# The second product of a SwiGLU block: 8 of 22 inner blocks plainly, 14 by seven block products in one group

## The chip, the cores and the metric

One core of one Trainium2 chip runs the whole kernel. The metric is the device time of one execution in microseconds (us); less is better. Engines are named as in the profile: PE (matmuls), PEld (weight loads of PE), DVE (VectorE), ACT (ScalarE), POOL, and SP, whose queue issues the DMAs here.

## The reference

The kernel computes one decoder layer on 512 tokens of width 1024, in float32: a SwiGLU half-step, a mixing stage (retention and block-sparse attention, one input projection, one output projection), and a second SwiGLU half-step. The half-steps are what matters here:

```python
FFN_DIM = 2816
def _swiglu(h, w_gate, w_up, w_down):
    return (jax.nn.silu(h @ w_gate) * (h @ w_up)) @ w_down
x = x + 0.5 * _swiglu(_rms(x, ffn1_norm_w[l]), ffn1_w_gate[l], ffn1_w_up[l], ffn1_w_down[l])
...
x = x + 0.5 * _swiglu(_rms(x, ffn2_norm_w[l]), ffn2_w_gate[l], ffn2_w_up[l], ffn2_w_down[l])
```

In blocks of 128, the model width is 8 blocks and the inner width 22. The **gate and up products** make the 22 inner blocks `hs[0..21]` (each 128 by 512 tokens); the **down product** multiplies them with `w_down` to 8 output blocks.

## The kernel before

Each float32 operand is split in two float32r parts, a rounded `h` (an ACT copy) and a remainder `lo` (a DVE subtraction). A product then takes three matmuls: h·h, h·lo and lo·h (`mm3`, and the inner loop of `strassen`). Weights are loaded as 256 KB tiles `raw` (four 128x128 blocks), and split into `wh` and `wl`.

`ffn` runs once at the start (FFN1) and once at the end (FFN2). Its first 6 inner blocks (`EVEN`) are computed plainly, with moving tiles of 512 tokens. The other 16 go in 8 calls of `hidden`, each for two inner blocks, with the block method of seven products (Strassen's in Winograd's form): the matrix of weights is cut in 2 by 2, the tokens in two halves of 256, and seven products of 256 columns replace eight. A product of `hidden` has 24 matmuls (two weights matrices, four blocks deep, three parts), a call 168. `token_blocks` prepares the token side once (sums and differences of the normed input, and their splits), `strassen` the weight side in each call. `weave` interleaves two calls in time, so that products of one stand between products of the other. The results stay in PSUM banks: bank `a` takes P1 and then, added on top, U2, U3 and C21; bank `b` takes P5 and later B; bank `c` takes P2. What a bank holds after a product must be read before the next product adds to it: ACT copies it (`taken`, into `keep`).

The down product, which is the part in question, is plain in this version: for each of 8 output blocks `db`, 22 inner blocks by 3 matmuls of 512 columns, 66 in all, into one bank of `p` or `s` in turn; at its end one DVE instruction adds half of it to the residual `y`. In FFN2 the last output block is cut in two halves of 256 columns. All 22 inner blocks are split (`parts`). `nxt` then passes `y` on: in FFN1 to `Stream.add`, which makes the next norm's operands (on ACT a scaled copy and a square, on DVE a remainder and a sum), in FFN2 to a DMA to the output.

All operations are first recorded by `Plan` (line 71) and then ordered per engine by its list scheduler (`_order`), with assumed costs (`_cost`) and limits on live tiles (`SLOTS`, `BANKS`, 98 slots in all). Nearly every instruction therefore carries line 196 in the profile, where the recorded call is made. Engines work their queues strictly in that order.

Of the kernel before, what the change touches and what calls it, by code (L numbers as in the profile page):

```python
# [27 lines left out]
F32R = mybir.dt.float32r  # L28
# [6 lines left out]
KB = 8  # L35
# [282 lines left out]
def tile_layer(ctx: ExitStack, tc: tile.TileContext, x_t, cols_in, wg1, wu1, wd1, w_int, w_inn,  # L318
# [22 lines left out]
    def f32(ap):  # L341
        return ap.bitcast(F32)
# [87 lines left out]
    class Stream:  # L430


        def __init__(self, nw):
            self.nw, self.parts, self.ssq = nw, [], None

        def add(self, kb, x, delay=0):
            self.part(kb, x)
# [2 lines left out]
        def part(self, kb, x):  # L440
            w = self.nw[:, kb:kb + 1]
            h, lo = slot(F32R), slot(F32R)
            nc.scalar.activation(h, x, AF.Copy, scale=w)
            nc.vector.scalar_tensor_tensor(lo, x, w, f32(h), op0=OP.mult, op1=OP.subtract)
            self.parts.append((h, lo))

        def square(self, x, delay=0):
            nc.delay = delay
# [16 lines left out]
    def token_blocks(pairs, gates=None):  # L465


        res = [[] for _ in range(7)]
        gate = lambda q: setattr(nc, "after", gates and gates[min(q, len(gates) - 1)])
        for q, (one, two) in enumerate(pairs):  # L470
            gate(q)
            if q % 2 == 0:
                bh, bl = slot(F32R, use="block"), slot(F32R, use="block")
            o = slice(256 * (q % 2), 256 * (q % 2) + 256)
            nc.scalar.activation(bh[:, o], one[:, :256], AF.Copy)
            nc.vector.tensor_sub(bl[:, o], one[:, :256], f32(bh[:, o]))
            res[0].append((bh[:, o], bl[:, o]))
# [24 lines left out]
        return res  # L502

    def strassen(load, nk, moving, taken):

        n = nk * 128
        r = {}
        for i, j in ((1, 1), (1, 2), (2, 1), (2, 2)):  # L510
            r[i, j] = [slot(use="raw")[:, :n] for _ in range(2)]
            for m in range(2):
                load(r[i, j][m], m, i, j)

        s1 = [slot(use="sum")[:, :n] for _ in range(2)]
        s = [s1, s1, r[2, 1], r[1, 2]]
        for m in range(2):
            nc.vector.tensor_add(s1[m], r[2, 1][m], r[2, 2][m])
        for m in range(2):
            nc.vector.tensor_sub(s[2][m], r[1, 1][m], r[2, 1][m])  # L520
        banks, marks = {}, []

        def product(tag, w, block, said):
            start = tag not in banks
            if start:
                banks[tag] = bank(tag)
            p = banks[tag]
            marks.append(len(nc.ops) + 2)
            for m in range(2):
                h, lo = slot(F32R, use="wh")[:, :n], slot(F32R, use="wl")[:, :n]  # L530
                nc.scalar.activation(h, w[m], AF.Copy)
                nc.vector.tensor_sub(lo, w[m], f32(h))
                out = p[:, 256 * m:256 * m + 256]
                for k in range(nk):
                    o = slice(k * 128, k * 128 + 128)
                    xh, xl = moving[block][k]
                    for a, (ww, xx) in enumerate(((h, xh), (h, xl), (lo, xh))):
                        nc.tensor.matmul(out, ww[:, o], xx, start=start and m + k + a == 0,
                                         stop=k == nk - 1 and a == 2, skip_group_check=True)
# [8 lines left out]
        for m in range(2):  # L548
            nc.vector.tensor_sub(s1[m], s1[m], r[1, 1][m])
        product("a", s[1], 4, "U2")  # L550
        for m in range(2):
            nc.vector.tensor_sub(s[3][m], r[1, 2][m], s1[m])
# [27 lines left out]
    def ffn(st, x, wg, wu, wd, nxt, was, first=None, last=False):  # L580
# [40 lines left out]
        def hidden(one, two):  # L621
            def load(t, m, i, j):
                nc.sync.dma_start(t.rearrange("p (a b) -> p a b", a=4),
                                  (wg, wu)[m][(one, two)[i - 1]][:, 4 * j - 4:4 * j])

            rows = [[slot(use="row") for _ in range(2)] for _ in range(2)]
            keep = {}

            def add(i, j, p, old):

                for m in range(2):
                    o = slice(256 * m, 256 * m + 256)
                    nc.vector.tensor_add(rows[i][m][:, 256 * j:256 * j + 256], p[:, o], old[:, o])

            def taken(what, p):
                if what in ("P1", "U2", "U3"):
                    keep[what] = slot(use="keep")
                    nc.scalar.activation(keep[what], p, AF.Copy)
                elif what == "P5":
                    keep[what] = p  # L640
                if what == "P2":
                    add(0, 0, p, keep["P1"])
                elif what == "U3":
                    add(1, 1, keep["P5"], keep["U3"])
                    g, u = (t[:, 256:] for t in rows[1])
                    nc.scalar.activation(g, g, AF.Silu)
                    hs[two] = slot()
                    nc.vector.tensor_mul(hs[two][:, 256:], g, u)
                elif what == "C21":
                    g = rows[1][0][:, :256]  # L650
                    nc.scalar.activation(g, p[:, :256], AF.Silu)
                    nc.vector.tensor_mul(hs[two][:, :256], p[:, 256:], g)
                elif what == "B":
                    add(0, 1, p, keep["U2"])
# [5 lines left out]
            return strassen(load, 4, blocks, taken)  # L660

        marks = weave([lambda _, q=q: hidden(q, q + HALF) for q in range(EVEN, EVEN + HALF)])

# [3 lines left out]
            x[db] = slot()  # L667
            nc.sync.dma_start(x[db], was[db])
        nc.after = None
        order = [*range(FB - 1 - HALF), *range(FB - HALF, FB - 1), FB - 1 - HALF, FB - 1]  # L670
        parts = {}
        for fb in order:
            parts[fb] = split(hs[fb])
        for db in range(KB):

            cuts = [(0, 256), (256, 512)] if last and db == KB - 1 else [(0, 512)]
            ps = [bank("ps"[(db + i) % 2]) for i in range(len(cuts))]
            wh, wl = split_w(wd[db], (128, FB, 128))
            y = x[db]
            for p, (a, b) in zip(ps, cuts):  # L680
                for n, fb in enumerate(order):
                    hh, hl = parts[fb]
                    mm3(p[:, a:b], wh[:, fb], wl[:, fb], hh[:, a:b], hl[:, a:b], n == 0, n == FB - 1)
                nc.vector.scalar_tensor_tensor(y[:, a:b], p[:, a:b], 0.5, y[:, a:b],
                                               op0=OP.mult, op1=OP.add)
                nxt(db, y, a, b)

# [413 lines left out]
```

## Time and profile before

| | us |
|---|---|
| median of 3 runs (970.16 to 970.73) | 970.26 |
| profiled execution, whole | 970.63 |
| its span | 968.8 |
| PE busy (99% of the span, 5676 matmuls) | 960.1 |
| PEld busy (88%) | 848.3 |
| DVE busy (71%) | 687.1 |
| ACT busy (53%) | 510.1 |

The share of a span is a mean over stages. A row of a view by time gives the start, the duration, the engine, what it did, and in brackets the idle time before it with what ended that. A group of like instructions that follow each other without a gap stands as one row with a count, under the shape of the first; the last of them ends at start plus duration. The granted clock of PE stands in the views by window as PEclk, in parts of full speed. About 2 us of the whole lie outside the span.

### The profile page before, as it was taken

The numbers are of one execution on the slowest core, as the hardware profiler recorded it, in microseconds if no ns is written. First come the engines' busy times: TensorE is split into PE (matmuls) and PEld (weight loads), VectorE is DVE, ScalarE is ACT, GpSimd is POOL, SyncE is SP. The second block draws the span as 40 slices with busy tenths as digits, with TensorE's granted clock in tenths as the row PEclk, the third lists the DMA queues.
The fourth block names the chain that finished last, engine by engine and source line by source line (L and its number), as shares of the span: only waits on it lengthen the run. The fifth ranks groups of instructions, "written<-read, shape, count | busy, mean of one in ns | idle before, by whom it ended". The sixth has DMA issues, their size and how long they took to land.

```text
span 968.8 us, 15318 instructions
## 1 busy us (share of the span) xinstructions
PE 960.1 (99%) x5676; PEld 848.3 (88%) x5676; DVE 687.1 (71%) x1333; ACT 510.1 (53%) x999; POOL 0.2 (0%) x4
## 2 busy tenths in 40 slices
PE   9999999999999999999999999999999999999998
PEld 6889999999888888888788878888999999988888
DVE  7997888997343344379989988798788899733130
ACT  7544558556232235369987975554445765542200
POOL 0000000000000000000000000000000000000000
PEclk9999999999999999999999999999999999999999
DMA  9413332337425641114405432811333133643200
GB/s 307 174 55 103 107 97 77 97 106 226 134 83 184 184 150 36 58 66 117 159 27 164 158 103 70 273 60 54 110 101 111 54 109 108 199 149 125 87 28 22
DMA packets 65099, 112.24 MB, mean 116 GB/s; under 512 B 8064, under 2 KB 13184, under 8 KB 65024
## 3 DMA queue, kind: packets, MB, share of 16 engines
q1 hardware_dynamic: 65024, 111.26, 36.3%
q8 instruction: 44, 0.72, 0.3%
q14 instruction: 31, 0.25, 0.1%
HBM read 101.79 MB, written 6.29 MB: 112 GB/s over the span
## 4 chain that ended last, share of the span: by engine, by line
PE 87%; ACT 6%; DVE 4%; DMA 1%; issue 1%; SPq 1%; DVEq 0%; ACTq 0%
PE ps L196 87%; ACT s L196 6%; DVE s L196 4%; DMA s<-in_w_int_dram 1%; SPq L196 1%; DMA s<-in_x_t_dram 0%; DVE c L196 0%; DVE ad L196 0%; DVEq L196 0%; ACTq L196 0%
## 5 line engine op out<-in xcount | busy, mean ns | idle before, releaser
L196 PE MATMUL ps<-s 128*128 128x256 f32 (+1 forms) x5506 | 944.9, 332 | 3.1 <-ACT s L196 1.9
L196 PEld LDWEIGHTS ps<-s 128*128 128x128 f32 x5506 | 828.8, 190 | 105.5 <-ACT s L196 6.6
L196 DVE TENSOR_TENSOR s<-s 128x512 fp32r<-128x512 f32 (+5 forms) x834 | 498.3, 652 | 58.7 <-ACT s L196 50.2
L196 ACT ACTIVATE s<-s 128x512 fp32r<-128x512 f32 (+2 forms) x700 | 383.9, 603 | 222.6 <-DVE s L196 144.9
L196 DVE TENSOR_TENSOR s<-ps,s 128x256 f32<-128x256 f32 (+5 forms) x216 | 103.3, 501 | 44.8 <-PE ps L196 25.8
L196 ACT ACTIVATE s<-ps 128x512 f32<-128x512 f32 (+7 forms) x148 | 75.7, 519 | 84.5 <-PE ps L196 78.3
L196 DVE SCALAR_TENSOR_TENSOR s<-ps,s 128x512 f32<-128x512 f32 (+1 forms) x17 | 11.2, 660 | 144.0 <-PE ps L196 144.0
L196 ACT ACTIVATE s<-s,cols 128x512 fp32r<-128x512 f32 x24 | 17.2, 722 | 77.4 <-DVE s L196 75.9
L196 DVE SCALAR_TENSOR_TENSOR s<-s,cols 128x512 fp32r<-128x512 f32 (+1 forms) x44 | 32.1, 747 | 9.2 <-ACT s L196 8.9
L196 DVE SCALAR_TENSOR_TENSOR s<-s 128x512 f32<-128x512 f32 x30 | 20.6, 686 | 9.2 <-ACT s L196 8.9
L196 ACT ACTIVATE s<-s,c 128x384 f32<-128x384 f32 (+3 forms) x32 | 20.7, 649 | 1.7 <-DVE c L196 1.5
L196 PE MATMUL ps<-ct,s 128*128 128x128 f32 x100 | 17.3, 278 | 1.3 <-ACT s L196 1.3
L196 PEld LDWEIGHTS ps<-ct,s 128*128 128x128 f32 x100 | 11.9, 140 | 5.5 <-ACT s L196 3.8
L196 DVE CUSTOM_DVE_ANT_0 s<-ps,s 128x384 f32<-128x384 f32 (+3 forms) x32 | 14.7, 483 | 0.5 <-PE ps L196 0.4
L196 ACT ACTIVATE s<-ps,cols 128x512 f32<-128x512 f32 x8 | 5.5, 683 | 17.0 <-PE ps L196 17.0
L196 PE MATMUL ps<-s,cr 128*128 128x512 f32 x30 | 11.8, 415 | 0.2 <-ACT s L196 0.2
L196 DVE SCALAR_TENSOR_TENSOR s<-ps,c,s 128x128 fp32r<-128x128 f32 (+1 forms) x24 | 8.2, 386 | 1.7 <-ACT s L196 1.7
L196 DVE SCALAR_TENSOR_TENSOR s<-s,ps 128x512 f32<-128x512 f32 x12 | 8.1, 678 | 0.6 <-PE ps L196 0.6
L196 PEld LDWEIGHTS ps<-s,cr 128*128 128x128 f32 x30 | 5.6, 188 | 3.0 <-ACT s L196 1.3
L196 ACT ACTIVATE s<-ps,c 128x256 fp32r<-128x256 f32 x16 | 6.3, 480 | 2.2 <-PE ps L196 2.2
L196 DVE TENSOR_SCALAR c<-c 128x1 f32<-128x1 f32 x32 | 6.4, 206 | 0.0
L196 ACT ACTIVATION_READ_ACCUMULATOR s<-s,c 128x1 f32 x32 | 6.2, 192 | 0.0
(29 smaller groups left out, 52.2 us busy)
## 6 DMA issues: line engine op xcount, KB each, us to landing
s<-in_wg_dram SPq DMA_DIRECT2D x87, 256.0 KB, 2.9
s<-in_wu_dram SPq DMA_DIRECT2D x87, 256.0 KB, 2.9
s<-in_wd_dram SPq DMA_DIRECT2D x80, 256.0 KB, 3.5
s<-in_w_int_dram SPq DMA_DIRECT2D x40, 256.0 KB, 4.0
s<-in_x_t_dram SPq DMA_DIRECT2D x16, 256.0 KB, 3.9
s<-in_rtab_dram SPq DMA_DIRECT2D x16, 256.0 KB, 3.0
s<-in_w_inn_dram SPq DMA_DIRECT2D x16, 256.0 KB, 3.9
s<-in_wd_dram SPq DMA_DIRECT2D x16, 128.0 KB, 2.9
```

The costliest lines, as they stand in the source:

```text
L196: self.ops.append([eng, cost, lambda: fn(*args, **kwargs), deps, tiles, i + self.delay + DELAYS.get(self.part, 0), self.part, shared])
```

## The change

The down product of both blocks is cut in two. The first 8 inner blocks (`PLAIN`) are multiplied plainly, 8 times 24 matmuls of 512 columns, and added to the residual. The other 14 (`PAIRED` is 7, paired as 8+k with 15+k) go through the block method: `token_blocks` makes seven sets of operands from 7 pairs of inner blocks, and four calls of `output`, one for two output blocks each, run `strassen`, woven like the calls of `hidden`. A product has one group of 7 blocks (in tiles of four and three), which is 21 matmuls of 256 columns. Its result is not kept: a DVE instruction adds plus or minus half of it straight from the bank to the residual. The signs inside `strassen` and `token_blocks` are turned so that all sums of weights are additions; `hidden` follows with negated copies. In FFN2 the output leaves in 16 DMAs of 256 columns.

```diff
+PLAIN = 8
+PAIRED = (22 - PLAIN) // 2
...
-    SLOTS = {"raw": 12, "sum": 4, "wh": 6, "wl": 6, "keep": 4, "row": 8, "block": 32}
+    SLOTS = {"raw": 12, "sum": 4, "wh": 6, "wl": 6, "keep": 4, "row": 8, "block": 52}
...
+        def negative(n, src, bh, bl, o):
+            nc.scalar.activation(bh[:, o], src, AF.Copy, scale=-1.0)
+            nc.vector.scalar_tensor_tensor(bl[:, o], src, -1.0, f32(bh[:, o]), op0=OP.mult, op1=OP.subtract)
+            res[n].append((bh[:, o], bl[:, o]))
...
-            two_blocks(1, two)
+            h, lo = slot(F32R, use="block"), slot(F32R, use="block")
+            nc.scalar.activation(h[:, :256], two[:, :256], AF.Copy)
+            nc.vector.tensor_sub(lo[:, :256], two[:, :256], f32(h[:, :256]))
+            res[1].append((h[:, :256], lo[:, :256]))
+            negative(2, two[:, 256:], h, lo, slice(256, 512))
...
-            nc.vector.tensor_sub(u[:, :256], two[:, 256:], one[:, 256:])
+            nc.vector.tensor_sub(u[:, :256], one[:, 256:], two[:, 256:])
...
-            for m in range(2):
-                h, lo = slot(F32R, use="wh")[:, :n], slot(F32R, use="wl")[:, :n]
+            for u, (n, k0, col) in enumerate(units):
+                h, lo = slot(F32R, use="wh")[:, :128 * n], slot(F32R, use="wl")[:, :128 * n]
...
-                    nc.scalar.activation(keep[what], p, AF.Copy)
+                    nc.scalar.activation(keep[what], p, AF.Copy, scale=1.0 if what == "U3" else -1.0)
...
-        order = [*range(FB - 1 - HALF), *range(FB - HALF, FB - 1), FB - 1 - HALF, FB - 1]
-        parts = {}
-        for fb in order:
-            parts[fb] = split(hs[fb])
+
+        parts = []
+        for fb in range(PLAIN):
+            nc.after = marks[-2]
+            parts.append(split(hs[fb]))
+        nc.after = None
         for db in range(KB):
...
+            wh, wl = split_w(wd[db, :, :PLAIN], (128, PLAIN, 128))
+            p, y = bank("ps"[db % 2]), x[db]
+            for fb in range(PLAIN):
+                mm3(p, wh[:, fb], wl[:, fb], *parts[fb], fb == 0, fb == PLAIN - 1)
+            nc.vector.scalar_tensor_tensor(y, p, 0.5, y, op0=OP.mult, op1=OP.add)
+        units = [(n, k0, 0) for k0, n in ((k, min(4, PAIRED - k)) for k in range(0, PAIRED, 4))]
+        blocks = token_blocks([(hs[PLAIN + k], hs[PLAIN + PAIRED + k]) for k in range(PAIRED)])
+
+        def output(db):
...
+            def taken(what, p):
+
+                i, j, sign = {"P1": (0, 0, -1), "P2": (0, 0, 1), "U2": (0, 1, -1), "B": (0, 1, -1),
+                              "U3": (1, 1, 1), "P5": (1, 1, 1), "C21": (1, 0, 1)}[what]
+                y, o = x[db + 4 * i], slice(256 * j, 256 * j + 256)
+                nc.vector.scalar_tensor_tensor(y[:, o], p[:, :256], 0.5 * sign, y[:, o],
                                                op0=OP.mult, op1=OP.add)
...
+            return strassen(load, units, blocks, taken)
+
+        weave([lambda _, db=db: output(db) for db in range(4)])
```

The scheduler moves more than the diff shows. On PE, around FFN1's down product, the order before is (names: `ps` a bank, `s` a slot; the shape is the output's):

```order
L196 MATMUL ps<-s 128x256 x1296
L196 MATMUL ps<-s 128x512 x7
L196 MATMUL ps<-s 128x256 x48
L196 MATMUL ps<-s 128x512 x541
```

and now, from the same place on:

```order
L199 MATMUL ps<-s 128x256 x1344
L199 MATMUL ps<-s 128x512 x192
L199 MATMUL ps<-s 128x256 x588
L199 MATMUL ps<-s 128x512 x20
```

The seven plain matmuls that stood inside the last call of `hidden`, between its U3 and its C21, are gone from there; the other 521 of the down product become 192 of 512 columns and 588 of 256, and the 20 matmuls of the mixing stage that followed them follow still. The order is the same in FFN2.

On DVE, in FFN1's block stage, from the sum over P1 of the second call on (`s_653` to `s_660` are the residuals; `ps_836` and `ps_845` are banks `a` and `c` of the second call, `ps_807` is bank `a` of the first):

```order
L199 SCALAR_TENSOR_TENSOR s_654<-ps_836,s_654 128x256
L199 TENSOR_TENSOR s_851<-s_803,s_850 128x512
L199 TENSOR_TENSOR s_853<-s_804,s_852 128x384
L199 TENSOR_TENSOR s_858<-s_799,s_857 128x512
L199 SCALAR_TENSOR_TENSOR s_657<-ps_807,s_657 128x256
L199 TENSOR_TENSOR s_860<-s_800,s_859 128x384
L199 TENSOR_TENSOR s_876<-s_825,s_875 128x512
L199 SCALAR_TENSOR_TENSOR s_654<-ps_845,s_654 128x256
L199 TENSOR_TENSOR s_878<-s_826,s_877 128x384
L199 TENSOR_TENSOR s_825<-s_825,s_817 128x512
L199 TENSOR_TENSOR s_826<-s_826,s_818 128x384
L199 TENSOR_TENSOR s_819<-s_819,s_825 128x512
```

A reading of a bank now stands behind two to four splits or sums of weights in the same queue, where before a plain down product had one reading for 66 matmuls.

On PE, at the end of the last call of FFN2 (`ps_2651` is its bank `a`, `ps_2673` its bank `b`), where no other call is left to stand between its products:

```order
L199 MATMUL ps_2651<-s_2513,s_2680 128x256
L199 MATMUL ps_2651<-s_2514,s_2680 128x256
L199 MATMUL ps_2651<-s_2513,s_2681 128x256
L199 MATMUL ps_2673<-s_2474,s_2690 128x256
L199 MATMUL ps_2673<-s_2475,s_2690 128x256
L199 MATMUL ps_2673<-s_2474,s_2691 128x256
L199 MATMUL ps_2673<-s_2476,s_2690 128x256
L199 MATMUL ps_2673<-s_2477,s_2690 128x256
L199 MATMUL ps_2673<-s_2476,s_2691 128x256
L199 MATMUL ps_2651<-s_2516,s_2682 128x256
L199 MATMUL ps_2651<-s_2517,s_2682 128x256
L199 MATMUL ps_2651<-s_2516,s_2683 128x256
```

Six matmuls of B stand between U2 and U3; eight more stand between U3 and C21, and seven come last.

## Rows read from the trace of the kernel before

**Rows 1.** Busy time by window: us, engines, granted clock, DMA share, GB/s.
```profile
core 0: us, PE busy (x) PEld busy (x) DVE busy (x) ACT busy (x) POOL busy (x), PEclk, DMA share, GB/s
100.00:150.00 50.00, 50.00 (x419) 50.00 (x418) 41.72 (x78) 26.72 (x51) 0.00 (x0) 1.00 0.32 98
250.00:300.00 50.00, 50.00 (x222) 41.38 (x222) 19.14 (x32) 15.69 (x30) 0.00 (x0) 1.00 0.36 103
```
**Rows 2.** Timeline of ACT, `hidden` of FFN1: the copies of U2, one per call.
```profile
85.47 0.60 ACT L196 ACTIVATE s<-ps 128x512 f32<-128x512 f32 x1 [4.69 <-PE ps L196]
...
105.63 0.60 ACT L196 ACTIVATE s<-ps 128x512 f32<-128x512 f32 x1 [2.54 <-PE ps L196]
...
125.85 0.60 ACT L196 ACTIVATE s<-ps 128x512 f32<-128x512 f32 x1 [2.60 <-PE ps L196]
```
**Rows 3.** Timeline of DVE, down product of FFN2: the readings of the banks.
```profile
875.24 0.69 DVE L196 SCALAR_TENSOR_TENSOR s<-ps,s 128x512 f32<-128x512 f32 x1 [10.93 <-PE ps L196]
...
890.20 0.69 DVE L196 SCALAR_TENSOR_TENSOR s<-ps,s 128x512 f32<-128x512 f32 x1 [10.93 <-PE ps L196]
...
957.96 0.42 DVE L196 SCALAR_TENSOR_TENSOR s<-ps,s 128x256 f32<-128x256 f32 x1 [6.89 <-PE ps L196]
965.87 0.42 DVE L196 SCALAR_TENSOR_TENSOR s<-ps,s 128x256 f32<-128x256 f32 x1 [7.49 <-PE ps L196]
```
**Rows 4.** Timeline, end of the last `hidden` call: FFN1, FFN1, FFN2.
```profile
226.59 0.60 ACT L196 ACTIVATE s<-ps 128x512 f32<-128x512 f32 x1 [1.46 <-PE ps L196]
...
227.24 122.95 PE L196 MATMUL ps<-s 128*128 128x256 f32 x575 [0.69 <-ACT s L196]
...
836.34 129.50 PE L196 MATMUL ps<-s 128*128 128x256 f32 x666 [0.74 <-ACT s L196]
```
**Rows 5.** Busy time by window, late in `hidden` of FFN1 (columns as in 1).
```profile
190.00:200.00 10.00, 10.00 (x86) 10.00 (x85) 10.00 (x20) 5.26 (x11) 0.00 (x0) 1.00 0.31 105
200.00:210.00 10.00, 10.00 (x86) 10.00 (x85) 10.00 (x19) 6.47 (x13) 0.00 (x0) 1.00 0.30 82
```
**Rows 6.** Timeline of DVE, same stretch: back to back instructions of 256 and 512.
```profile
194.91 0.76 DVE L196 TENSOR_TENSOR s<-ps,s 128x256 f32<-128x256 f32 x2
195.58 3.69 DVE L196 TENSOR_TENSOR s<-s 128x512 fp32r<-128x512 f32 x6
...
201.40 12.12 DVE L196 TENSOR_TENSOR s<-s 128x512 fp32r<-128x512 f32 x20
```
**Rows 7.** Timeline of DVE, one output block of FFN1's down product.
```profile
266.13 0.69 DVE L196 SCALAR_TENSOR_TENSOR s<-ps,s 128x512 f32<-128x512 f32 x1 [9.34 <-PE ps L196]
266.74 0.42 DVE L196 TENSOR_TENSOR s<-s 128x256 fp32r<-128x256 f32 x1
267.61 0.75 DVE L196 SCALAR_TENSOR_TENSOR s<-s,cols 128x512 fp32r<-128x512 f32 x1 [0.46 <-ACT s L196]
268.28 3.69 DVE L196 TENSOR_TENSOR s<-s 128x512 f32<-128x512 f32 x6
```
**Rows 8.** Groups by line and shape: names, shapes, count; busy us, mean ns; idle.
```profile
L196 DVE TENSOR_TENSOR s<-s 128x512 fp32r<-128x512 f32 x525 | 338.4, 683 | 56.8 <-ACT s L196 49.3 <-issue 4.9 <-PE ps L196 2.0
L196 ACT ACTIVATE s<-s 128x512 fp32r<-128x512 f32 x525 | 301.2, 621 | 124.5 <-DVE s L196 68.5 <-PE ps L196 51.1 <-DMA s<-s 2.3
L196 DVE TENSOR_TENSOR s<-s 128x256 fp32r<-128x256 f32 x42 | 17.2, 416 | 0.1
L196 DVE TENSOR_TENSOR s<-ps,s 128x384 fp32r<-128x384 f32 x20 | 10.9, 550 | 0.1
```
**Rows 9.** Timeline of DVE, just ahead of FFN1's `hidden`.
```profile
73.96 0.69 DVE L196 TENSOR_TENSOR s<-ps,s 128x512 f32<-128x512 f32 x1 [1.38 <-PE ps L196]
```
**Rows 10.** DMA issues, the larger loads of `w_down`: count, KB each, us to landing.
```profile
s<-in_wd_dram SPq DMA_DIRECT2D x80, 256.0 KB, 3.5
```
**Rows 11.** Timeline of the output DMAs, and the last window (columns as in 1).
```profile
958.41 8.25 SPq L196 DMA_DIRECT2D out_dram<-s  x2
...
965.87:968.80 2.93, 0.00 (x0) 0.00 (x0) 0.42 (x1) 0.00 (x0) 0.00 (x0) 1.00 0.13 45
```

More of the change, by code (lines that the diff above doesn't have):

```diff
@@ L433, in __init__ @@
         def __init__(self, nw):
-            self.nw, self.parts, self.ssq = nw, [], None
+            self.nw, self.parts, self.ssq = nw, {}, None
         def add(self, kb, x, delay=0):
@@ L502, in token_blocks, with strassen @@
         return res
-    def strassen(load, nk, moving, taken):
-        n = nk * 128
-        r = {}
+    def strassen(load, units, moving, taken):
+        r, us = {}, range(len(units))
         for i, j in ((1, 1), (1, 2), (2, 1), (2, 2)):
-            r[i, j] = [slot(use="raw")[:, :n] for _ in range(2)]
-            for m in range(2):
-                load(r[i, j][m], m, i, j)
-        s1 = [slot(use="sum")[:, :n] for _ in range(2)]
+            r[i, j] = [slot(use="raw")[:, :128 * n] for n, _, _ in units]
+            for u in us:
+                load(r[i, j][u], u, i, j)
+        s1 = [slot(use="sum")[:, :128 * n] for n, _, _ in units]
         s = [s1, s1, r[2, 1], r[1, 2]]
[L517 to L520, printed above, removed]
+        for u in us:
+            nc.vector.tensor_add(s1[u], r[2, 1][u], r[2, 2][u])
+        for u in us:
+            nc.vector.tensor_add(s[2][u], r[1, 1][u], r[2, 1][u])
         banks, marks = {}, []
@@ L528, in product @@
             marks.append(len(nc.ops) + 2)
-            for m in range(2):
-                h, lo = slot(F32R, use="wh")[:, :n], slot(F32R, use="wl")[:, :n]
[L531 to L534, printed above, removed]
+            for u, (n, k0, col) in enumerate(units):
+                h, lo = slot(F32R, use="wh")[:, :128 * n], slot(F32R, use="wl")[:, :128 * n]
+                nc.scalar.activation(h, w[u], AF.Copy)
+                nc.vector.tensor_sub(lo, w[u], f32(h))
+                out = p[:, col:col + 256]
+                for k in range(n):
                     o = slice(k * 128, k * 128 + 128)
-                    xh, xl = moving[block][k]
+                    xh, xl = moving[block][k0 + k]
                     for a, (ww, xx) in enumerate(((h, xh), (h, xl), (lo, xh))):
-                        nc.tensor.matmul(out, ww[:, o], xx, start=start and m + k + a == 0,
-                                         stop=k == nk - 1 and a == 2, skip_group_check=True)
+                        nc.tensor.matmul(out, ww[:, o], xx, start=start and u + k + a == 0,
+                                         stop=k == n - 1 and a == 2, skip_group_check=True)
             taken(said, p)
@@ L547, in strassen @@
         product("b", s[0], 3, "P5")
-        for m in range(2):
-            nc.vector.tensor_sub(s1[m], s1[m], r[1, 1][m])
+        for u in us:
+            nc.vector.tensor_add(s1[u], s1[u], r[1, 1][u])
         product("a", s[1], 4, "U2")
-        for m in range(2):
-            nc.vector.tensor_sub(s[3][m], r[1, 2][m], s1[m])
+        for u in us:
+            nc.vector.tensor_add(s[3][u], r[1, 2][u], s1[u])
         yield marks
@@ L627, in hidden, with add @@
             keep = {}
-            def add(i, j, p, old):
+            def add(i, j, p, old, op=OP.add):
                 for m in range(2):
                     o = slice(256 * m, 256 * m + 256)
-                    nc.vector.tensor_add(rows[i][m][:, 256 * j:256 * j + 256], p[:, o], old[:, o])
+                    nc.vector.tensor_tensor(rows[i][m][:, 256 * j:256 * j + 256], p[:, o], old[:, o], op=op)
             def taken(what, p):
@@ L653, in taken @@
                 elif what == "B":
-                    add(0, 1, p, keep["U2"])
+                    add(0, 1, keep["U2"], p, OP.subtract)
                     g, u = rows[0]
@@ L658, in taken @@
                     nc.vector.tensor_mul(hs[one], g, u)
-            return strassen(load, 4, blocks, taken)
+            return strassen(load, [(4, 0, 0), (4, 0, 256)], blocks, taken)
         marks = weave([lambda _, q=q: hidden(q, q + HALF) for q in range(EVEN, EVEN + HALF)])
@@ new lines, in ffn, with load @@
+        blocks = token_blocks([(hs[PLAIN + k], hs[PLAIN + PAIRED + k]) for k in range(PAIRED)])
+        def output(db):
+            def load(t, u, i, j):
+                n, k0, _ = units[u]
+                f = PLAIN + (j - 1) * PAIRED + k0
+                nc.sync.dma_start(t.rearrange("p (a b) -> p a b", a=n), wd[db + 4 * (i - 1), :, f:f + n])
+            def taken(what, p):
[3 more added lines that the diff above has]
+                nc.vector.scalar_tensor_tensor(y[:, o], p[:, :256], 0.5 * sign, y[:, o],
+                                               op0=OP.mult, op1=OP.add)
+                if last and what in ("P2", "B", "U3", "C21"):
+                    nxt(db + 4 * i, y, o.start, o.stop)
+                elif not last and what in ("B", "C21"):
+                    nxt(db + 4 * i, y, 0, 512)
+            return strassen(load, units, blocks, taken)
```

17 lines of the change are left out of this document (2 added, 15 removed).

## The prediction

> **What bounds the kernel now.** I read the busy time by window first. Early in `hidden` PE is busy for all of 50 us at the full granted clock, and DVE for 42 of the 50 [rows 1]; in FFN1's plain down product PE is just as full and DVE idle for 31 of 50. So both stages last as long as their matmuls, and the clock, at its upper level of 2.4 GHz throughout, plays no part. The timeline then gives the price of a matmul. In `hidden` the copies of U2 of three successive calls start 40.38 us apart [rows 2]; for 2 calls of 168 matmuls of 256 columns that is 0.120 us each. In the down product two readings of a bank are 14.96 us apart [rows 3], 0.2267 us for each of 66 matmuls of 512 columns; the 66 of 256 columns at the very end take 7.91 us, 0.120 each again. A wide matmul is thus 6% cheaper per column than two narrow ones. Last, the end of the last `hidden` call: PE stands still for 0.69 us in FFN1 and 0.74 us in FFN2 while ACT copies U2 out of bank `a` for 0.60 us [rows 4], as U3 is added to the same bank.
>
> **The matmuls.** FFN1's down product has 528 wide matmuls, 8 times 14.96 or 119.7 us. FFN2's has 7 times 14.96 and twice 7.91, 120.5 us. The change puts 192 wide ones (192 x 0.2267 = 43.5 us) and 588 narrow ones (4 calls x 7 products x 21, at 0.120: 70.6 us) in place of each, 114.1 us. That takes off 5.6 and 6.4 us, **12.0 us** in all, if PE stays full. By columns it would be 8%; the narrow form eats almost half of it.
>
> **The gaps at the end of `hidden`.** Seven plain matmuls covered the copy of U3 before; the order now has U2, U3 and C21 with nothing between them. The gap that rows 4 show once per block then comes twice. Its price is bounded below by the copy alone, 0.60 us, and above by twice the gap, where the copy stands behind other work in ACT's queue; I take the gap as measured, 0.69 + 0.74 = **1.4 us** more.
>
> **DVE in `hidden`.** The preparation of the 7 pairs begins there. Instructions that follow each other start 0.606 us apart at 512 elements (12.12 us for 20) and 0.335 at 256 (195.58 less 194.91, halved) [rows 6]. From the first sums of weights to the last inner block the order has 215 of the first and 65 of the second before, 204 and 97 now: 152 us become 156, of 1344 x 0.120 = 161.3 us of PE. Late in the stage DVE was already busy for all of the time and PE lost nothing [rows 5], so this costs nothing; if it were not covered it would be the 4 us per block. The four pieces of the token side that `hidden` itself now splits in halves add 4 x 0.07 us on DVE, and DVE waits 1.38 us for PE shortly before they matter [rows 9]: nothing.
>
> **DVE in the plain part.** From the end of `hidden` to the first split of the block stage it has 33 instructions of 512, 16 of 256 and 3 of 384 elements. One of 384 lies between the other two forms, in start to start as in duration (550 ns) [rows 8]; I take 0.47. That makes 20.1 + 5.4 + 1.4 = 26.9 us, beside 43.5 us of PE. Covered, with 16 us to spare; the readings of the plain products (0.61 us each [rows 7]) are in it.
>
> **DVE in the block stage.** A call has 7 splits and 4 sums of weights, each of 512 and 384 elements, 11 x 1.08 = 11.8 us, and 7 readings of 256 at 0.34 (their 0.42 us [rows 3] less the 0.08 by which instructions overlap [rows 7]), 2.4 us: 14.2 us beside 147 x 0.120 = 17.64 us of PE. In FFN1 two output blocks per call go on to the norm, each a remainder of 0.67 and a sum of 0.61 [rows 7]: 16.8 us. DVE is covered in both, but in FFN1 by 0.8 us a call only. Two instructions of 256 cost 0.67 where one of 512 costs 0.606, so cutting the work into narrow pieces is dear by a tenth, and it is in these prices.
>
> The Trainium skill speaks against such pieces more strongly: "VectorE: DVE Perf Modes", section "The TRN2 errata", says that an instruction pays a fixed cost whatever its size, and to work on at least 512 elements. It gives N + 151 cycles at 0.96 GHz for a float32 sum: 424 and 691 ns, where this trace has durations of 416 and 683. The rule holds here for durations; the starts in rows 6 show part of the fixed cost hidden behind the next instruction. What follows if it is not hidden is the first rival.
>
> **ACT, the queues, the tail.** ACT has 14 copies per call, at most 14 x 0.62 us [rows 8] = 8.7 of 17.64 us. The loads of `w_down` keep their number (48) and bytes, in 16 of 256 KB plainly, then 16 of 256 and 16 of 192 KB where there were 40 of 256 and 8 of 128; at about 3.5 us to landing [rows 10] and twelve `raw` tiles they have tens of us of lead. SP issues seven more output DMAs in FFN2, each well under 1 us, while PE works. After the last matmul a reading of 0.42 us and one DMA remain, 2.93 us before [rows 11]; a second DMA leaves 0.8 us (7 matmuls) ahead of it, for which I add 0.2. The mixing stage between the blocks keeps its order on PE, ACT and DVE; its 20 first matmuls cover the last norm operands as before.
>
> **Sum.** -12.0 + 1.4 + 0.2 = -10.4 us. Against the profiled execution (970.63, span 968.8) that is 960.2; the median lies 0.37 lower, so **959.9 us**.
>
> **Rival 1: DVE sets the pace in FFN1.** If its instructions do not overlap, they cost their durations: 7 x (0.683 + 0.55) + 4 x 1.23 + 7 x 0.42 + 2 x (0.75 + 0.68) = 19.4 us a call, 1.7 over PE's 17.64, 6.9 us in four calls: 966.8. The rule of "VectorE: DVE Perf Modes" above, taken at its word, says this. Rows 6 speak against it. For a milder form speaks that early in `hidden` DVE has, by the prices of rows 6, 16.6 us of work per call (22 splits and sums, 6 readings, 3 multiplications) and idles some 3.4 us of 20.2 [rows 1], in waits for PE and ACT; 0.8 us a call is less than that. Against it: late in the stage the idle time shrinks to nothing without a loss [rows 5]. Between 959.9 and 966.8 I put it at 963.3, chance 0.15.
>
> **Rival 2: exposed banks, slower than before.** U2, U3 and C21 are each added to bank `a` once DVE has read what stands there: 3 changes of hands a call, 24 in all. ACT did this before, with an engine half idle; now the reading stands in DVE's queue behind splits. It is hidden as long as it ends within the product of the other call that stands between, 21 x 0.120 = 2.52 us (0.7 us in the last call, six matmuls of B). DVE works in order and idles 10.93 us ahead of a reading that PE has not finished [rows 3], so a split placed ahead of a reading, late for its weights, would hold PE. If every change of hands showed as the 0.69 us of rows 4, 24 of them would cost 16.6 us: 976.5. Against it: with two splits (1.1 us) and the reading (0.42) it still ends 1 us early. The Trainium skill ("TensorE: Matmul & The Clock Gate", "Architectural detail") calls DVE's queue a strict FIFO; the trace agrees. Chance 0.05.
>
> **Numbers.** Forecast 0.77, rival 1 0.15, rival 2 0.05; 0.03 for a disturbance of the mixing stage that eats the gain. A measurement of this kernel tells about 0.2%, 2 us, from no change. Faster 0.92, same 0.03, slower 0.05. The range goes from 958.2, where the extra gaps and the tail cost nothing (970.26 - 12.0), to 963.6, which holds the milder half of rival 1.
>
> **What would show it.** Right: PE without a gap from the first plain matmul of a down product to the last of its block stage, 5.44 us between readings in the plain part (24 matmuls), 17.6 us from call to call after it, and two stops of about 0.7 us in the last `hidden` call. DVE busy about 8 of 10 us in FFN2's block stage and above 9 of 10 in FFN1's. Rival 1 would show calls of 18 us and more in FFN1 alone, with PE waiting for DVE's splits; rival 2 short stops of PE before U2, U3 or C21 in both blocks. The prediction is wrong if PE waits in the block stage for more than 1 us a call, or if the narrow matmul takes more than 0.120 us there.

## The result

| | before | after |
|---|---|---|
| median, same chip (us) | 970.5 (970.16 to 972.38, 4 runs) | 962.13 (961.4 to 963.12, 4 runs) |
| profiled execution, span | 970.63, 968.8 | 961.62, 959.8 |
| PE busy, matmuls | 960.1, 5676 | 948.3, 6114 |
| DVE busy | 687.1 (71%) | 802.2 (84%) |
| ACT busy | 510.1 (53%) | 548.4 (57%) |

The ratio is 0.9912, with a 95% interval from 0.99 to 0.9925: 8.4 us faster. 959.9 was forecast, 958.2 to 963.6 as the range. The direction and the mechanism came out, and 2.0 us of the 10.4 that were forecast did not come (the other 0.2 us between 962.13 and 959.9 come from the median of before, 970.5 here and 970.26 in the forecast).

**Where the time went.** Three landmarks in the two traces divide it. From the first copy of U2 [rows 2] (85.47 before, 84.98 after) to the last reading of a bank [rows 3] (965.87, 956.81) it is 880.40 us before and 871.83 after: 8.57 us less. The 0.49 us that the first landmark itself lies earlier come from the loads at the start, which the change does not touch; in the traces of this study that landmark lies between 84.98 and 86.48. All experiments below are therefore also compared by this **interval**, first copy of U2 to last reading. The copy of U2 in the last `hidden` call of FFN1 lies 0.50 earlier (226.59 before [rows 4], 226.09 after), which is the start alone, so `hidden` up to there lasts as long as before. The whole gain and the whole loss lie between that copy and the end of a down product, twice.

The chain that ended last, from the page of the kernel after:

```profile
PE 80%; DVE 11%; ACT 7%; issue 1%; DMA 1%; SPq 0%; DVEq 0%; ACTq 0%
```

The same line of the page of the kernel before:

```profile
PE 87%; ACT 6%; DVE 4%; DMA 1%; issue 1%; SPq 1%; DVEq 0%; ACTq 0%
```

That DVE now holds 11% of the chain instead of 4% is the first sign of what the forecast had not seen.

**The plain part and the block stage.** DVE's timeline of the kernel after; two readings of the plain part, and the sums over P1 of two successive calls in FFN1, against [rows 3]:

```profile
264.44 0.69 DVE L199 SCALAR_TENSOR_TENSOR s<-ps,s 128x512 f32<-128x512 f32 x1
...
269.88 0.69 DVE L199 SCALAR_TENSOR_TENSOR s<-ps,s 128x512 f32<-128x512 f32 x1 [0.79 <-PE ps L199]
...
300.91 0.42 DVE L199 SCALAR_TENSOR_TENSOR s<-ps,s 128x256 f32<-128x256 f32 x1
...
318.55 0.42 DVE L199 SCALAR_TENSOR_TENSOR s<-ps,s 128x256 f32<-128x256 f32 x1
```

Plain readings are 5.44 us apart, which is 24 x 0.2267; calls are 17.64 us apart, which is 147 x 0.120. Both are the forecast numbers. The windows of the plain part, of the block stages of FFN1 and FFN2, and of one call in FFN1, against [rows 1]:

```profile
core 0: us, PE busy (x) PEld busy (x) DVE busy (x) ACT busy (x) POOL busy (x), PEclk, DMA share, GB/s
236.92:280.73 43.81, 43.81 (x197) 36.30 (x196) 34.55 (x64) 18.24 (x32) 0.00 (x0) 1.00 0.39 125
280.73:351.75 71.02, 70.83 (x589) 70.62 (x589) 61.80 (x121) 34.87 (x67) 0.00 (x0) 1.00 0.50 156
886.00:956.77 70.77, 70.77 (x589) 70.55 (x587) 52.66 (x105) 23.93 (x49) 0.00 (x0) 1.00 0.27 86
...
318.50:336.20 17.70, 17.70 (x150) 17.70 (x149) 16.88 (x35) 9.82 (x18) 0.00 (x0) 1.00 0.65 213
```

PE is full in all of them, at the full granted clock. DVE is busy for 61.80 of 71.02 us in FFN1's block stage and for 16.88 of 17.70 in one of its calls, and PE loses 0.19 us to it, once.

**The stops.** PE's timeline of the kernel after: every stop in or beside a down product. These answer to [rows 4].

```profile
226.74 3.13 PE L199 MATMUL ps<-s 128*128 128x256 f32 x24 [0.69 <-ACT s L199]
231.16 112.79 PE L199 MATMUL ps<-s 128*128 128x256 f32 x767 [1.29 <-ACT s L199]
344.14 12.14 PE L199 MATMUL ps<-s 128*128 128x256 f32 x81 [0.19 <-DVE s L199]
...
832.20 3.13 PE L199 MATMUL ps<-s 128*128 128x256 f32 x24 [0.69 <-ACT s L199]
836.61 120.16 PE L199 MATMUL ps<-s 128*128 128x256 f32 x828 [1.29 <-ACT s L199]
```

The first stop of each pair, between U2 and U3, was there before. The second, between U3 and C21, is new, and it lasts 1.29 us, not the 0.69 and 0.74 that were carried over from [rows 4]. ACT's timeline at that place tells why:

```profile
226.09 0.60 ACT L199 ACTIVATE s<-ps 128x512 f32<-128x512 f32 x1 [0.92 <-PE ps L199]
226.80 0.63 ACT L199 ACTIVATE s<-s 128x512 fp32r<-128x512 f32 x1
228.41 2.22 ACT L199 ACTIVATE s<-s 128x512 fp32r<-128x512 f32 x4 [0.97 <-DVE s L199]
230.53 0.58 ACT L199 ACTIVATE s<-ps 128x512 f32<-128x512 f32 x1
```

The copy of U3 (230.53) could have started when U3 ended, at 229.87 (226.74 + 3.13). It stands in ACT's queue behind four splits, and the first of those had waited 0.97 us for DVE. In the kernel before, ACT stood idle until U3 ended and copied at once:

```profile
230.40 0.60 ACT L196 ACTIVATE s<-ps 128x512 f32<-128x512 f32 x1 [2.18 <-PE ps L196]
```

The chain of waits of the kernel after (its longest pieces) leads from there back through DVE:

```profile
8.88 165.36 PE ps L199 x1118
174.26 5.80 DVE s L199 x11
...
225.39 3.00 DVE s L199 x7
228.41 1.02 ACT s L199 x2
229.48 1.64 ACT s L199 x3
231.16 99.97 PE ps L199 x660
```

For 54 us, from 174 to 228, the end of the program hangs on DVE: on the sums for the 7 pairs and the splits of `hidden`, piece upon piece. In that time PE stops once, for the 0.69 us of U2's copy, and otherwise has matmuls in stock; the bill comes at the first place where it has none.

### The profile page after: what moved, and what is told of

The parts are those of the page before. It is cut to its first block, busy times and chain, and to the rows that moved or that the text cites. A ratio compares the mean times of both kernels' runs of the same rounds, so it can differ in the third digit from the quotient of the medians.

```text
span 959.8 us, 16650 instructions
## 1 busy us (share of the span) xinstructions
PE 948.3 (99%) x6114; PEld 859.4 (90%) x6114; DVE 802.2 (84%) x1606; ACT 548.4 (57%) x1097; POOL 0.2 (0%) x4
## 4 chain that ended last, share of the span: by engine, by line
PE 80%; DVE 11%; ACT 7%; issue 1%; DMA 1%; SPq 0%; DVEq 0%; ACTq 0%
PE ps L199 80%; DVE s L199 11%; ACT s L199 7%; DMA s<-in_w_int_dram 0%; DMA s<-in_x_t_dram 0%; SPq L199 0%; DVE ad L199 0%; DVE c L199 0%; DVEq L199 0%; ACT c L199 0%; ACTq L199 0%
## 5 line engine op out<-in xcount | busy, mean ns | idle before, releaser
L199 PE MATMUL ps<-s 128*128 128x256 f32 (+2 forms) x5944 | 933.1, 318 | 5.8 <-ACT s L199 4.6
L199 PEld LDWEIGHTS ps<-s 128*128 128x128 f32 x5944 | 839.9, 191 | 85.2 <-ACT s L199 8.7
L199 DVE TENSOR_TENSOR s<-s 128x512 fp32r<-128x512 f32 (+5 forms) x1008 | 587.4, 640 | 53.5 <-ACT s L199 42.9
L199 ACT ACTIVATE s<-s 128x512 fp32r<-128x512 f32 (+4 forms) x798 | 422.7, 586 | 261.7 <-DVE s L199 209.5
L199 DVE TENSOR_TENSOR s<-ps,s 128x256 f32<-128x256 f32 (+6 forms) x184 | 92.1, 522 | 39.2 <-PE ps L199 24.2
L199 DVE SCALAR_TENSOR_TENSOR s<-ps,s 128x256 f32<-128x256 f32 (+1 forms) x72 | 34.8, 483 | 35.3 <-PE ps L199 34.8
L199 DVE SCALAR_TENSOR_TENSOR s<-s 128x256 fp32r<-128x256 f32 (+1 forms) x74 | 39.0, 535 | 9.1 <-ACT s L199 8.9
L199 DVE TENSOR_TENSOR s<-s,ps 128x256 f32<-128x256 f32 x32 | 12.1, 426 | 0.0
```

The lines of the kernel that those rows point to most:

```text
L199: self.ops.append([eng, cost, lambda: fn(*args, **kwargs), deps, tiles, i + self.delay + DELAYS.get(self.part, 0), self.part, shared])
```

## The experiments

The theory after the result: the 2.0 us are mostly the second stop, 1.29 instead of about 0.7, twice, because the preparation of the pairs fills DVE and with it ACT's queue. Its rivals: the readings and splits in the block stage (rivals 1 and 2 of the prediction) cost something that single stops do not show. The median of before on the same chip was 970.54 for e1 to e4, 970.87 for e5 to e8, 970.60 for e9 and e10.

### e1: let the plain matmuls fill the stops again

```diff
         for fb in range(PLAIN):
-            nc.after = marks[-2]
+            nc.after = marks[0]
             parts.append(split(hs[fb]))
```

`marks[-2]` is the first matmul of C21 in the last `hidden` call: the operands of the plain part are not split before it, so no plain matmul can stand ahead of C21. With `marks[0]` seven of them stand between U3 and C21, as before the change.

> The splits of the eight plain inner blocks may start at P1 of the last hidden call instead of at its C21; the order then has seven plain matmuls between U3 and C21 again. Theory (C21 waits for ACT's copy of U3, which stands behind splits that wait for DVE, and nothing covers it): the stop of 1.29 us before C21 goes in both blocks, 7 x 0.227 = 1.6 us of plain work fill it: 2.6 us less than the change, 959.5 us, ratio to the kernel before 0.9886. Rival (DVE is simply behind at the end of hidden, and the lost time turns up wherever the splits stand): no gain over the change, 962 us, the stop moved to another product.

Measured: 960.81 us (960.5 to 961.77), ratio 0.9903 (0.9889 to 0.9916); the interval is 870.11, 1.72 less than after. PE's timeline in FFN1 (FFN2 has 0.69 and 0.28):

```profile
227.54 3.61 PE L199 MATMUL ps<-s 128*128 128x256 f32 x26 [0.69 <-ACT s L199]
231.43 112.36 PE L199 MATMUL ps<-s 128*128 128x512 f32 x765 [0.27 <-DVE s L199]
```

The stop of 1.29 is gone; in its place the third plain matmul (128x512) waits 0.27 us for DVE: of the three parts it is the first that needs the remainder `wl` of its weights. So 1.3 us of the 2.6 that were expected came by the medians, and the rival, no gain, did not. The rows give 2 x 1.02 = 2.04 us, the interval 1.72; 0.2 us of the difference are lost just before U2 ends, where a weight load (PEld, 225.41) waits 0.15 us for DVE and no idle row of PE shows it.

### e2: keep the fill out, take the pair work off DVE

```diff
-        blocks = token_blocks([(hs[PLAIN + k], hs[PLAIN + PAIRED + k]) for k in range(PAIRED)])
+        blocks = token_blocks([(hs[PLAIN + k], hs[PLAIN + PAIRED + k]) for k in range(PAIRED)], gates=[marks[-2]])
```

> The preparation of all seven pairs waits for C21 of the last hidden call. Theory (the copy of U3 is late because DVE is busy with the pairs): the stop before C21 falls from 1.29 to about 0.7 us in both blocks; but the 18 us of DVE work on five pairs move behind hidden, 27 + 18 = 45 us beside 43.5 + 5.8 us of PE, so P1 of the first call may wait 0 to 2 us. In all 961 to 965 us. Rival (the copy is late for ACT's own order or a DMA): the stop stays at 1.3 us.

Measured: 961.33 us (960.5 to 962.47), ratio 0.9907 (0.9894 to 0.9921); the interval is 870.58, 1.25 less than after. PE's timeline in FFN1, then ACT's:

```profile
230.75 112.79 PE L199 MATMUL ps<-s 128*128 128x256 f32 x767 [0.75 <-ACT s L199]
```

```profile
230.10 0.60 ACT L199 ACTIVATE s<-ps 128x512 f32<-128x512 f32 x1 [2.24 <-PE ps L199]
```

Now ACT waits 2.24 us for U3 to end, where before C21 waited for ACT, and the stop is 0.75, near the price that the prediction had taken. Twice 0.54 us is 1.08 of the 1.25. So the length of the second stop came from the pair work: **shown**. The chain of waits runs through PE and ACT alone at this place, and DVE's share of the whole chain falls from 11% to 4%. P1 of the block stage, for which 0 to 2 us were expected, does not wait.

### e3: the four calls of `output` one after the other

```diff
-        weave([lambda _, db=db: output(db) for db in range(4)])
+        for db in range(4):
+            for _ in output(db):
+                pass
```

> The four calls of the block stage follow each other and are not woven: between U2 and U3 stand 6 matmuls of B (0.72 us), between U3 and C21 nine (1.08 us), in place of 2.52 us of another call. Theory (a reading of 0.42 us is mostly in time, DVE has 3 us of slack a call in FFN2 and 0.8 in FFN1): stops of 0 to 0.5 us at 16 changes of hands, 962 to 967 us. Rival 2 of the prediction (each uncovered change of hands shows as about 0.69 us or more, behind one or two splits): 16 x 0.7 to 1.2 us, 971 to 981 us.

Measured: 964.35 us (963.87 to 965.45), ratio 0.9939 (0.9926 to 0.9951); the interval is 874.08, 2.25 more than after. PE's timeline, the two largest stops in FFN1's block stage (those in FFN2's are 0.16 and 0.15):

```profile
328.52 17.89 PE L199 MATMUL ps<-s 128*128 128x256 f32 x147 [0.33 <-DVE s L199]
346.78 12.15 PE L199 MATMUL ps<-s 128*128 128x256 f32 x81 [0.37 <-DVE s L199]
```

Without the other call only a call's own products stand between what is added to bank `a`, and even so no change of hands shows as 0.69 us. Rival 2 needed 24 of those. The four stops are 1.01 us, against the one of 0.19 in after; with what stands beside a stop (below, 0.25 us each) they make 1.6 of the 2.25 us that the weave is worth.

### e4: seven more instructions on DVE in each call

```diff
+    scratch = const.tile([128, 512], F32, name="scratch")
...
                 nc.vector.scalar_tensor_tensor(y[:, o], p[:, :256], 0.5 * sign, y[:, o],
                                                op0=OP.mult, op1=OP.add)
+                nc.vector.tensor_add(scratch, y, y)
```

> One further DVE instruction of 512 elements into a scratch tile after each of the 7 readings of a call, whose result nobody uses: 7 x 0.606 = 4.2 us a call. Theory (DVE costs 16.8 us a call in FFN1 and 14.2 in FFN2 by starts, beside 17.64 of PE): 21.0 and 18.4 us, so FFN1 loses up to 3.4 x 4 = 13.4 and FFN2 up to 0.8 x 4 = 3.2 us, less what DVE is ahead after the plain part: 974 to 979 us, call to call about 21.0 us in FFN1 and 18.4 in FFN2. Rival 1 of the prediction (instructions cost their durations, 19.4 and 16.5 us a call): 24.2 and 21.3 us a call, 995 to 1003 us.

Measured: 973.95 us (972.35 to 975.31), ratio 1.0037 (1.0023 to 1.005). The statistics of the norm behind FFN1 start at 369.36 instead of 357.25, 11.9 us later once the start (85.22 against 84.98) is taken off; from there to the last reading it is 599.48 us, against 599.56 after. Six wide matmuls of the mixing stage (1.4 us) stand ahead of these statistics in e4 and behind them in after, so FFN1 paid for about 10.5 us and FFN2, with the same 28 instructions of 0.606 us (17 us), for about 1.3, with two stops of 0.20 and 0.18 us at its end. PE's timeline in FFN1's block stage, and two windows there (columns as above):

```profile
329.51 19.16 PE L199 MATMUL ps<-s 128*128 128x256 f32 x145 [3.65 <-DVE s L199]
350.50 17.89 PE L199 MATMUL ps<-s 128*128 128x256 f32 x108 [1.82 <-DVE s L199]
```

```profile
303.00:321.00 18.00, 17.63 (x145) 17.22 (x144) 17.72 (x35) 8.32 (x17) 0.00 (x0) 1.00 0.28 78
321.00:339.00 18.00, 14.05 (x101) 13.57 (x101) 16.87 (x33) 8.40 (x17) 0.00 (x0) 0.91 0.59 177
```

This is the mechanism of rival 1 made real in FFN1, where DVE's starts add up to 21.0 us a call beside PE's 17.64. It does not come call by call as expected: counted in matmuls of PE, the second, third and fourth call of FFN1 begin 17.6, 18.5 and 23.8 us after the one before, and those of FFN2 17.6 to 17.7. DVE is ahead after the plain part and the debt comes due late, in FFN2 hardly at all; at which load DVE begins to pace a call is not shown. Of FFN1's 10.5 us the stops are 5.9 (0.27, 0.30, 3.65 and 1.82, less the 0.19 of after); about 2.8 are a lower clock behind the two long ones (last section), for which the expectation had no term, so it is in part luck that the sum came to the edge of its range. The run does decide between starts and durations as the price of DVE's work: 973.95 us, against 974 to 979 by the one and 995 to 1003 by the other. The Trainium skill ("VectorE: DVE Perf Modes", "The TRN2 errata") gives the fixed cost per instruction, and durations here agree with it (416 and 683 ns [rows 8]); for a queue that runs full the distance between starts is what counts.

### e6 and e5: both remedies, then the weights of the fill as well

e6 has the edits of e1 and e2. e5 adds one:

```diff
+            nc.delay = -250 if db == 0 else 0
             wh, wl = split_w(wd[db, :, :PLAIN], (128, PLAIN, 128))
+            nc.delay = 0
```

which places the load and the splits of the first plain output block 250 numbers earlier (the scheduler goes by an operation's number in the recorded order).

> The first and the second experiment together, without the weights pulled ahead: plain splits from P1 on, pairs from C21 on. Theory: the stop before U3 stays at 0.69 us, the one before C21 goes entirely (0.28 us was left when the pairs were still in the way): 2.6 us less than the change, 959.5 us. Rival: as in the first experiment, 960.8 us.

> The splits of the plain inner blocks from P1 of the last hidden call on, the weights of the first plain output block ahead of other work, and the pairs prepared only from C21 of that call on. The order then has seven plain matmuls (1.59 us) both between U2 and U3 and between U3 and C21. Theory: both stops (0.69 and 1.29 us) go in both blocks, 4.0 us less than the change, 958.2 us, ratio 0.9873. Rival (DVE is behind, the lost time moves on, to P1 of the block stage): stops of 1 to 2 us at P1, 960 to 962 us.

Measured: e6 958.96 us (958.74 to 959.17), ratio 0.9877 (0.9863 to 0.989), interval 868.79. e5 957.39 us (956.98 to 957.52), ratio 0.986 (0.9846 to 0.9873), interval 866.83. In e6 one stop of 0.69 us is left in each block; the interval is 3.04 less than after, where the second stops alone are 2.58. In e5 no stop is left but the 0.20 us in FFN1's block stage: seven plain matmuls stand in each of the two gaps, and their weights are there. Both are 0.5 to 0.8 us faster than their theories, which counted the idle rows alone: a stop costs some 0.25 us more (below).

### e10: the early weights without the gate on the pair work

> e5 without its gate on the pair work: e1 plus the weights of the first plain output block 250 numbers earlier. The fill between U3 and C21 then finds its weights split, so the two waits of 0.28 us that e1 had there go: 960.81 less 0.56, 960.2. The pair work stands again where e1 has it, so the gain of e5 over this run, if it is 2 us or more, is the gain of gating the pair work (e6 against e1 gave 1.85). If the early weights alone give 959 or less, then the weights, not the pair work, were what held e1 back from 958.

Measured: 957.35 us (956.96 to 957.46), ratio 0.9861 (0.9848 to 0.9873), interval 867.13. The expectation (960.2) failed and the other reading held: the early weights do it alone. They let plain matmuls stand before U3 too, which e1 could not, and then PE waits for no copy. The chain of waits in the stretch where after had hung on DVE and ACT is one piece:

```profile
214.95 25.16 PE ps L199 x185
```

ACT's timeline, the copies of U2 and U3:

```profile
229.68 0.60 ACT L199 ACTIVATE s<-ps 128x512 f32<-128x512 f32 x1 [0.21 <-PE ps L199]
...
234.21 0.60 ACT L199 ACTIVATE s<-ps 128x512 f32<-128x512 f32 x1 [1.68 <-PE ps L199]
```

Where PE has other work at hand, the pair work on DVE costs nothing (957.35 against 957.39 in e5); e2's remedy is then not needed. But both copies come at once here: ACT waits for PE ahead of them, as it does for 1.69 us ahead of U3's in e1. With the fill in place ACT's queue has another order, too: the copy was late only where the pair work met the order without the fill (after), and no run shows what a late copy costs behind a filled gap. This and e5 are the fastest kernels of the study, 0.5% below the changed one (ratios to before of 0.9861 and 0.986, against 0.9912).

### e7 and e8: ten and six plain blocks, with the edit of e1

```diff
-PLAIN = 8
+PLAIN = 10
```

and for e8 `PLAIN = 6`, with `"block": 60` in place of 52 for one more pair.

> The first experiment with 10 plain inner blocks and 12 by the block method (products of 6 blocks, in tiles of four and two). By matmuls 48 wide ones (10.9 us) replace 84 narrow ones (10.1 us) per block: 1.6 us more in all. DVE has a call of 12.7 us in FFN2 and 15.3 in FFN1 beside 15.1 of PE, so FFN1 is on the edge: 0 to 1 us more. 962.4 to 963.5 us. Rival (DVE's work is what holds the change back): less pair work, no slower than the first experiment, 959 to 961 us.

> The first experiment with 6 plain inner blocks and 16 by the block method (products of 8 blocks, two tiles of four; 60 slots for the token side). By matmuls 1.6 us less in all. DVE has 15.7 us a call in FFN2 and 18.3 in FFN1 beside 20.16 of PE, more slack than with 14 blocks, but one more pair (3.6 us) and 10.9 us less of plain matmuls to prepare under. Theory: 959.2 us, up to 961 if P1 has to wait. Rival (DVE's work holds the change back): 963 us and more, with PE waiting for DVE in the plain part.

Measured: e7 962.11 us (961.47 to 963.19), ratio 0.991 (0.9897 to 0.9924), 1.30 over e1. Two inner blocks are 48 wide matmuls (10.88 us) or 84 narrow ones (10.08), 0.80 us per block of the layer, 1.6 in all: the price of the forecast, tested at another size. 962.11 is just under the expected 962.4 to 963.5, and the rival, no slower than e1, did not come. e8 970.53 us (969.43 to 972.13), ratio 0.9998 (0.9989 to 1.0007): the expectation failed by 10 us and the gain of the whole change is gone. PE's timeline of e8 shows one long stop in each block:

```profile
227.67 42.64 PE L199 MATMUL ps<-s 128*128 128x256 f32 x222 [0.69 <-ACT s L199]
274.15 87.80 PE L199 MATMUL ps<-s 128*128 128x256 f32 x688 [3.85 <-DVE s L199]
...
883.89 81.67 PE L199 MATMUL ps<-s 128*128 128x256 f32 x666 [3.85 <-DVE s L199]
```

They stand where the block stage begins, not in the plain part as the rival had it. The windows of e8 around the first of them, from the plain part on (columns as above):

```profile
237.60:270.30 32.70, 32.70 (x150) 27.11 (x149) 28.55 (x62) 18.41 (x34) 0.00 (x0) 1.00 0.46 155
...
270.30:274.20 3.90, 0.05 (x2) 0.05 (x1) 3.90 (x8) 1.82 (x3) 0.00 (x0) 0.88 0.47 134
...
276.00:278.00 2.00, 2.00 (x12) 2.00 (x11) 1.71 (x3) 0.00 (x0) 0.00 (x0) 0.50 0.00 0
```

With two inner blocks less the plain part is 11 us shorter, and DVE has one pair more to prepare. It gets 28.55 us of work done in 32.70, where it had 37.28 in 43.80 in e1; the other 4.15 us it waits in the order of its queue, mostly for PE. What is left over comes when the plain part is over. DVE's timeline of e8 there:

```profile
269.81 0.68 DVE L199 SCALAR_TENSOR_TENSOR s<-ps,s 128x512 f32<-128x512 f32 x1
270.41 7.30 DVE L199 TENSOR_TENSOR s<-s 128x512 fp32r<-128x512 f32 x12
```

The last plain reading is at 269.81; the sums of weights and the splits of P1 are among the 12 instructions after it, while PE stands. Then comes a second bill: PE runs at a granted clock of 0.50, the lower of its two levels, until 280. PE's timeline, 27 matmuls behind the stop and 27 later, at the full clock:

```profile
274.15 6.10 PE L199 MATMUL ps<-s 128*128 128x256 f32 x27 [3.85 <-DVE s L199]
...
280.81 3.40 PE L199 MATMUL ps<-s 128*128 128x256 f32 x27
```

That is 2.7 us more, of which 2.4 go to the clock and the rest stands beside any stop. (The counts in a window of 2 us hold matmuls that lie in it in part.) Two stops of 3.85 us with 0.25 beside each, 2.4 us lost to the clock behind the first and 1.5 behind the second (16 matmuls in 3.58 us) are 12.1; less 1.6 for the matmuls, 0.4 for e1's waits of 0.27 and 0.28, which are below 0.1 here, and 0.45 for the late stop in FFN1, which e8 does not have, 9.7. The interval is 9.59 longer than e1's.

### e9: e8 with P1's weights ahead of the last readings

```diff
-            return strassen(load, units, blocks, taken)
+            return strassen(load, units, blocks, taken, -100 if db == 0 else 0)
...
+                nc.delay = early if (i, j) == (1, 1) else 0
                 load(r[i, j][u], u, i, j)
+                nc.delay = 0
...
+        nc.delay = early
         product("a", r[1, 1], 0, "P1")
+        nc.delay = 0
```

> Six plain blocks as in e8, with the loads and the splits of P1 of the first output call placed 100 numbers earlier, so that its splits of the weights stand on DVE ahead of the last two plain readings and not behind the last one and four weight sums. If the 3.85 us stop of e8 at the start of the block stage came from where P1's splits stand in DVE's queue, it goes, and with it the stretch of 6 us at a granted clock of 0.5 behind it in FFN1 (3.0 us lost) and of 3.4 us in FFN2 (1.8 us): 970.5 less 12.5, so 957.5 to 959.5, which is also e1 less 1.6 for the matmuls. If DVE, busy 38.5 of 42.6 us in the plain part, simply has no time for the work, the stop only moves: another product or a plain block waits for a split, and the time stays above 964.

Measured: 968.06 us (964.8 to 969.62), ratio 0.9969 (0.9958 to 0.998). The stop moved and shrank, it did not go. PE's timeline of e9:

```profile
227.71 45.53 PE L199 MATMUL ps<-s 128*128 128x256 f32 x246 [0.69 <-ACT s L199]
276.32 83.81 PE L199 MATMUL ps<-s 128*128 128x256 f32 x664 [3.07 <-DVE s L199]
```

PE now stops 24 matmuls later than in e8 (246 of them since the last stop instead of 222), one product further on; FFN2 has the same stop of 3.07 us. So the second reading holds in what it forecast: the stop moves to another product, and the time stays above 964. Its reason, that DVE simply has no time for the work, is not shown: in the plain part of e8 DVE stands idle for 4.15 us, more than the stop of 3.85, mostly because its queue has next what PE has not finished. Whether another order, with the pair work later than P1 and P2, would use that time was not tried.

## Why the prediction was right, and where it was off

**The matmuls** (-12.0 us): right. 5.44 and 17.64 us stand in the trace, and e7 finds the same prices at another size.

**The gaps at the end of `hidden`** (+1.4 us): the step that was mis-sized. "I take the gap as measured" carried over a gap in which ACT was free at once. The prediction named the condition under which it would be longer, "where the copy stands behind other work in ACT's queue", and had no row for it; the pair work that the change puts into DVE just there makes that work late. It measured 2.58 us, inside the upper bound that the prediction gave (twice the gap) and not at the value that it took. To that comes about 0.25 us per stop that no idle row shows: 24 matmuls between two stops take 3.13 us where 24 x 0.120 are 2.88 (a matmul lasts longer than the 0.120 us after which the next one starts, and ahead of a stop there is no next one), and e5, which loses four stops of 3.96 us together, is 5.00 us shorter in its interval, e10 4.70. For the two new stops that is 0.5 us.

**DVE in `hidden`** ("this costs nothing"): right as far as the copy of U2, wrong as a statement on the stage. The copy of U2 is not late. But the argument from [rows 5], that DVE is full without a loss, held only because PE had matmuls in stock; the chain of waits shows DVE at its base for 54 us, and the cover ends where the last call has nothing between its products.

**DVE in the plain part**: right that it is covered. The 26.9 us were low: 34.55 are busy in the window, partly pair work that the sum had placed in `hidden`. The 16 us to spare were 9, and e8 shows that less is not enough in this order: with two plain blocks less, PE stops.

**DVE in the block stage and rival 1**: right that starts, not durations, are the price, and that 0.8 us a call is enough; the loss is one stop of 0.19 us. In FFN1 DVE is busy for 9.5 of 10 us in one call and for 8.7 over the stage, in FFN2 for 7.4 where "about 8" was forecast. e4 shows that the rival's mechanism exists: with seven more instructions a call it costs FFN1 10 us. With how many it begins was not measured.

**Rival 2**: refuted by e3, where even single calls keep their changes of hands covered to within 0.4 us.

**The tail** (+0.2): from the last reading to the end of the span it is 2.99 us, before 2.93 [rows 11]; the seven additional output DMAs cost nothing else.

**The account** over the interval, in which before is 880.40: -12.0 for the matmuls, +2.58 for the second stops, +0.19 for the wait in FFN1, +0.75 for what stands beside these three stops, -0.05 because FFN2's first stop is 0.69 instead of 0.74. That is -8.5; measured -8.57.

**The range.** That 962.13 lies inside 958.2 to 963.6 is in part luck: the upper end was set for half of rival 1, DVE as the pace of the block stage, and what used that room was the gaps, for which the range had no margin of their own.

## What to carry to other kernels

A busy engine off the critical path is covered only while the engine that it serves has other work in its queue: before calling such work free, look for the next place where the order has nothing to put in between, and price the stop there with the late engine's queue, not with a stop from a time when that engine was idle. The cheapest remedy here was to have independent matmuls ready at that place, operands and weights both (e10: 4.8 us below the changed kernel by medians), rather than to move the late work (e2: 0.8). When a cheaper form of the work also shortens the stage that hides its preparation, as from eight plain blocks to six, the limits meet suddenly: where 1.6 us of gain over e1 were expected, e8 lost 9.7.

## What was not expected of the hardware

The granted clock can fall during or behind a stop of PE, and the loss behind the stop can be nearly as large as the stop. In e8 a stop of 3.85 us was followed by a clock of 0.50 (1.2 GHz instead of 2.4) until 5.9 us behind its end, a loss of 2.4. In e4 a stop of 1.82 us was followed by 0.50 as well, a loss of about 1.4 by the prices of e8. PE's windows of e4, whose stops of 3.65 and 1.82 us end at 329.51 and 350.50:

```profile
329.50:331.50 2.00, 1.99 (x12) 0.72 0.00 0
331.50:333.50 2.00, 2.00 (x12) 0.50 0.45 130
...
350.50:352.50 2.00, 2.00 (x10) 0.59 0.59 194
352.50:354.50 2.00, 2.00 (x11) 0.55 0.53 150
```

(Columns: PE busy with its matmuls, granted clock, DMA share, GB/s.) Behind the two stops of after, 0.69 and 1.29 us, the clock stayed at 1.00. It does not fall alike in every execution: in e9 the mean granted clock was 1.000 once, with 964.8 us, and 0.995 to 0.998 otherwise, with 967.0 to 969.6.
